# Weight rounding, decay shift and key factor of the input projection on ScalarE instead of GpSimd

## The chip, the cores and the metric

The kernel runs on one core of one Trainium2 chip. The core has a matrix engine (TensorE, PE in the profile, with its weight loads PEld in a row of their own), VectorE (DVE), ScalarE (ACT), GpSimd (POOL), and SyncE (SP), which here only issues DMAs. The metric is the device time of one execution in microseconds.

## The reference

One layer of a hybrid diffusion backbone on 128 context tokens and 1024 latent tokens, model width 1024. All of it is float32:

```python
h = rmsnorm(x, ln1_g) * (1 + sc1) + sh1
r, k, v, xw, xa, xg, xb, gb = split(h @ w_in)
decay = exp(-0.6065 * sigmoid(w0 + tanh(xw) @ w_up))   # for two directions
a     = sigmoid(a0 + xa @ a_up)                        # for two directions
kk    = unit_norm_per_head(k * k_k)
k_dir = k * (1 + (a - 1) * k_a)
ya = rwkv7_scan(r, decay, kk, kk * a, k_dir, v)        # 8 heads x 64, both directions
yb = rglru_scan(conv(xb)) * gelu(gb)                   # 8 blocks x 64, both directions
x  = x + g1 * (concat(ya, yb) @ w_out)
x  = x + g2 * ((gelu(ua) * ub) @ w_down)               # ua, ub = conv(rmsnorm(x) ... @ w_up)
```

## The kernel before

All 1152 tokens are handled as one sequence of columns. A float32 product is made of three matrix products (`mm3`): each operand is split into a part rounded to the matrix engine's narrower format (`hi`, made by `round_hi`) and the rest (`lo`, made by `rest_lo`), and hi·hi, hi·lo and lo·hi are added up.

**Input projection.** The columns of `w_in` are taken in 22 tiles of 128 columns, in the order of the list `ORDER`: 12 (xw and xa), then the tiles of k, r and v in turn, three tiles of the gate, and later those of the LRU. `win_load` fetches a tile as two pieces `win` of 128x512; `win_parts` (line 702) makes `winp`, hi and lo, from each piece, with one `round_hi` and one `rest_lo` of 128x512. `winp` has two buffers. `wtile` prepares tile i+1 when tile i begins, so its roundings wait until the last matrix product of tile i-1 has read its buffer. `proj` then runs 3 x 8 x 3 products per tile over three spans of 384 tokens, into two PSUM banks, which ScalarE empties.

**Beside it** run several generators, stepped by `beside` at set rates between pieces of 12 products. `stage_ab(f)`, for each of four head pairs f, works on six groups: two directions of a piece of 128 tokens and twice 512. A group goes through `rates` (two small products, two tanh on ScalarE into `b1` and `s`), `keys`, `powers` (two exponentials on ScalarE), `scaled_keys` (four products on VectorE), and `products` (the small matrix products `dg`, emptied by ScalarE). `keys`, the function that the diff touches, does in its order: shift of the decay `s` (0.5 s + 0.5), factor of the keys `kd` (b1 times a per-partition number plus another), `b1` on VectorE, `kd` times k on GpSimd, and the running sum of `s` on VectorE. `inverse` (lines 497 and 499) is a chain of some 60 short VectorE products for each f; `unit_keys` norms the keys.

The order of the instructions on each engine is fixed when the program is built: a planner goes through them by their place in the program and by its own estimates of when operands are ready. So the order on an engine can differ from the program's; on GpSimd the factor `kd` (line 596) mostly stands ahead of the shift of `s` (line 595). Each engine then works through its own list strictly in turn, and waits at an instruction whose operands or buffer aren't ready.

After the groups and inverses end, at about 460 us, a second stage runs the recurrence in two lanes beside the rest of the projection (`rest_of_projection`), then come the output projection and the feed-forward network.

Of the kernel before, what the change touches and what calls it, by code (L numbers as in the profile page):

```python
# [10 lines left out]
AF = mybir.ActivationFunctionType  # L11
OP = mybir.AluOpType
# [46 lines left out]
def tile_hybrid_step(  # L59
# [9 lines left out]
    V, A, G, PE = nc.vector, nc.scalar, nc.gpsimd, nc.tensor  # L69
# [33 lines left out]
    def round_hi(eng, hi, src):  # L103

        if eng is A:
            A.activation(hi, src, AF.Copy)  # L106
        else:
            eng.tensor_scalar(hi, src, 1.0, 0.0, op0=OP.mult, op1=OP.add)  # L108

    def rest_lo(eng, lo, src, hi):  # L110

        eng.tensor_tensor(lo, src, hi.bitcast(F32), op=OP.subtract)  # L112

    def vhalf(n, d):

        return n if d == 0 else 1 - n
# [4 lines left out]
    def const(name, *shape):  # L121
        return cp.tile(list(shape), F32, name=name)
# [60 lines left out]
    def ag(name):  # L183
        return abp.tile([128, 512], F32, name=name, tag="ag", bufs=NAG)
# [11 lines left out]
    def x8(name, dt=F32):  # L196
        return s1.tile([128, 2, D], dt, name=name, tag="x8", bufs=2)
# [50 lines left out]

    ln_half = const("ln_half", 128, 1)
    V.memset(ln_half, -0.6931471805599453)  # L250
    hsel = const("hsel", 128, 2)
    V.memset(hsel, 0.0)
    V.memset(hsel[0:64, 0:1], 1.0)
# [34 lines left out]
    def col(name, i, n=1):  # L288
        o = off[name] + i
        return colA[:, o:o + n]  # L290
# [5 lines left out]
    def scaled(name, src, n, mul, add=0.0):  # L296
        t = const(name, 128, n)
        V.tensor_scalar(t, src, mul, add, op0=OP.mult, op1=OP.add)
        return t

    nka = scaled("nka", col("rw_k_a", 0, 4), 4, -1.0)
    oka = scaled("oka", nka, 4, 1.0, 2.0)
# [102 lines left out]
    for b in range(4):  # L405
# [7 lines left out]
        for m in (2 * b, 2 * b + 1):  # L413
            ht = t4("ht")
            for q, (a, e) in enumerate(((0, 128), (128, T))):
                A.activation(ht[:, a:e], xT[b][:, m % 2, a:e], AF.Identity, scale=A1[:, m, q:q + 1],
                             bias=modc[:, m, q:q + 1])
# [138 lines left out]
    def stage_ab(f):  # L556
# [4 lines left out]
        class Group:  # L561
# [30 lines left out]
            def keys(self):  # L592
                W, b1, s = self.W, self.b1, self.s
                self.kd = ag("kd")[:, 0:W]
                G.tensor_scalar(s, s, 0.5, 0.5, op0=OP.mult, op1=OP.add)
                G.tensor_scalar(self.kd, b1, nka[:, f:f + 1], oka[:, f:f + 1], op0=OP.mult, op1=OP.add)
                V.scalar_tensor_tensor(b1, b1, -1.0, self.kk, op0=OP.add, op1=OP.mult)
                G.tensor_tensor(self.kd, self.kd, self.k, op=OP.mult)
                V.tensor_tensor_scan(s, keep[:, 0:W], s, 0.0, op0=OP.mult, op1=OP.add)
# [55 lines left out]
        for tg, (a, b) in enumerate(((0, 128), (128, 640), (640, T))):  # L655
            data = []
            for src in (r_d, k_d, kk_d):
                t = ag("rk")[:, 0:b - a]
# [43 lines left out]
    def win_parts(raw):  # L702
        w = x8("winp", F32R)
        hi, lo = w[:, 0], w[:, 1]
        for i, t in enumerate(raw):
            c = slice(512 * i, 512 * i + 512)
            round_hi(G, hi[:, c], t)
            rest_lo(V, lo[:, c], t, hi[:, c])
        return [a.rearrange("p (k c) -> p k c", k=8) for a in (hi, lo)]

    def wtile(m):
        i = ORDER.index(m)
        for a, q in enumerate(ORDER[i:i + 3]):
            if q not in win_raw:
                win_raw[q] = win_load(q)
            if a < 2 and q not in win_q:
                win_q[q] = win_parts(win_raw[q])
        return win_q[m]
# [294 lines left out]
    for h in range(2):  # L1013
        r = half(h)
        for d in range(2):
            for n in range(2):
                s = vhalf(n, d)
# [713 lines left out]
    if True:  # L1731
# [17 lines left out]
        f = zf.rearrange("p i k t -> p (i k t)")  # L1749
# [108 lines left out]
```

## Time and profile before

| | |
|---|---|
| median of 3 runs | 1878.95 us (1877.78 to 1882.11) |
| profiled execution, time | 1878.41 us |
| profiled execution, span | 1876.7 us |
| mean granted TensorE clock | 0.943 |
| PE busy | 1740.1 us (93%) |
| DVE busy | 1286.3 us (69%) |
| ACT busy | 814.9 us (43%) |
| POOL busy | 793.0 us (42%) |

Busy time is summed over the span. PE counts as busy while products overlap in its pipeline. [...]

### The profile page before, as it was taken

What the parts mean: (1) busy time and instruction counts of PE and PEld (TensorE: products, weight loads), DVE (VectorE), ACT (ScalarE), POOL (GpSimd) and SP (SyncE); (2) the same over time, 40 slices, a digit from 0 to 9 for tenths busy, and PEclk for the clock granted to TensorE, in tenths of its full rate; (3) what the DMA queues carried; (4) which work ended last, traced back from release to release, by engine and by line L of the source; (5) the groups of instructions that cost most, each with busy time, mean ns of one, the idle gap of its engine ahead of it and who ended that gap; (6) DMA issues with size and microseconds to landing.
All of it is one profiled execution on the core that took longest, in us unless ns stands there. A gap on an engine that the chain in (4) does not pass through costs nothing.

```text
span 1876.7 us, 35779 instructions
## 1 busy us (share of the span) xinstructions
PE 1740.1 (93%) x13341; PEld 1458.6 (78%) x13341; DVE 1286.3 (69%) x2632; ACT 814.9 (43%) x1695; POOL 793.0 (42%) x834
## 2 busy tenths in 40 slices
PE   5989998988899999789997889999999999999996
PEld 4766676778778778456675689999999999788885
DVE  6456977788466774357778966667776678566764
ACT  6344544441466567334334854444444443121211
POOL 2053636432253554131112076666666664334340
PEclk8897889888999999899998989999999999999998
DMA  9243535442434333676776312222222225648581
GB/s 295 62 155 124 159 124 175 132 150 81 144 101 143 112 104 97 218 234 216 248 236 222 130 53 84 76 71 77 71 71 78 76 71 165 188 150 271 167 256 59
DMA packets 268429, 264.93 MB, mean 141 GB/s; under 512 B 21173, under 2 KB 218448, under 8 KB 268256
## 3 DMA queue, kind: packets, MB, share of 16 engines
q1 hardware_dynamic: 252496, 245.97, 41.6%
q10 hardware_dynamic: 15472, 16.54, 2.6%
q8 instruction: 105, 1.72, 0.4%
q14 instruction: 68, 0.56, 0.1%
q0 software_dynamic: 288, 0.14, 0.0%
HBM read 188.00 MB, written 74.58 MB: 140 GB/s over the span
## 4 chain that ended last, share of the span: by engine, by line
PE 70%; DVE 12%; issue 6%; DMA 4%; ACT 4%; POOL 3%; SPq 0%; ACTq 0%; POOLq 0%; DVEq 0%
PE acc L92 13%; PE mm L92 10%; PE x L92 7%; PE y L92 7%; PE z L92 7%; PE v L92 3%; PE wo L92 3%; PE md L92 2%; PE lg L92 2%; PE ya L92 2%; DVE gt L497 2%; DVE X L499 2%; PE pa L92 2%; PE yb L92 1%; PE ca L92 1%
## 5 line engine op out<-in xcount | busy, mean ns | idle before, releaser
L92 PE MATMUL mm<-h_hi,winp 128*128 128x384 f32 x1056 | 315.0, 369 | 4.4 <-DVE vr L806 3.0
L92 PEld LDWEIGHTS mm<-h_hi,winp 128*128 128x128 f32 x1056 | 206.9, 204 | 26.3 <-issue 15.5
L92 PE MATMUL mm<-h_lo,winp 128*128 128x384 f32 x528 | 193.8, 367 | 2.9 <-DVE h_lo L112 2.9
L112 POOL TENSOR_TENSOR wl<-raw,wh 128x512 fp32r<-128x512 f32 x110 | 154.2, 1404 | 69.8 <-ACT wh L106 69.8
L106 ACT ACTIVATE wh<-raw 128x512 fp32r<-128x512 f32 x110 | 69.3, 632 | 146.7 <-PE z L92 80.4
L92 PEld LDWEIGHTS mm<-h_lo,winp 128*128 128x128 f32 x528 | 107.6, 204 | 10.9 <-issue 5.1
L92 PE MATMUL x<-f_hi,wh 128*128 128x256 f32 (+1 forms) x352 | 106.0, 301 | 8.7 <-ACT q L1650 5.0
L1088 POOL TENSOR_TENSOR BK<-BK,pc 128x256 f32<-128x256 f32 x72 | 47.4, 660 | 154.7 <-PE pa L92 56.7
L92 PE MATMUL x<-f_lo,wh 128*128 128x256 f32 (+1 forms) x352 | 105.7, 300 | 0.2 <-DVE f_lo L112 0.2
L92 PE MATMUL x<-f_hi,wl 128*128 128x256 f32 (+1 forms) x352 | 105.5, 300 | 0.0
L92 PE MATMUL y<-t_hi,wh 128*128 128x320 f32 (+1 forms) x352 | 105.0, 298 | 0.4 <-DVE q L1655 0.4
L92 PE MATMUL y<-t_lo,wh 128*128 128x320 f32 (+1 forms) x352 | 104.8, 298 | 0.0
L92 PE MATMUL y<-t_hi,wl 128*128 128x320 f32 (+1 forms) x352 | 104.7, 298 | 0.0
L112 POOL TENSOR_TENSOR wl<-S,wh 128x512 fp32r<-128x512 f32 x44 | 57.9, 1315 | 105.1 <-ACT wh L106 105.1
L108 POOL TENSOR_SCALAR winp<-win 128x512 fp32r<-128x512 f32 x44 | 31.9, 740 | 151.3 <-PE mm L92 104.6
L92 PE MATMUL acc<-f_hi 128*128 128x512 f32 x330 | 90.2, 395 | 2.5 <-ACT zf L1758 2.5
L108 POOL TENSOR_SCALAR t_hi<-raw 128x512 fp32r<-128x512 f32 x66 | 55.2, 839 | 78.5 <-PE acc L92 37.4
L1617 DVE SCALAR_TENSOR_TENSOR zf<-C,fcw,zf 128x567 f32<-128x567 f32 x66 | 63.7, 964 | 24.0 <-ACT zf L1615 24.0
L92 PEld LDWEIGHTS x<-f_hi,wh 128*128 128x128 f32 x352 | 68.1, 193 | 9.7 <-ACT q L1650 5.6
L92 PEld LDWEIGHTS acc<-f_hi 128*128 128x128 f32 x330 | 62.7, 191 | 16.0 <-ACT zf L1758 2.9
L112 DVE TENSOR_TENSOR t_hi<-raw,t_hi 128x512 fp32r<-128x512 f32 x66 | 48.3, 738 | 36.1 <-POOL t_hi L108 36.1
L1615 ACT ACTIVATE zf<-C,colB,fcw 128x576 f32<-128x576 f32 x66 | 57.2, 867 | 30.8 <-DVE C L1687 16.9
(514 smaller groups left out, 5248.5 us busy)
## 6 DMA issues: line engine op xcount, KB each, us to landing
raw<-in_w_down SPq DMA_DIRECT2D x132, 256.0 KB, 3.2
raw<-in_w_up SPq DMA_DIRECT2D x88, 256.0 KB, 3.0
wmod<-in_w_mod SPq DMA_DIRECT2D x68, 256.0 KB, 4.2
act_d<-zf SPq DMA_DIRECT2D x44, 288.0 KB, 2.3
src<-act_d SPq DMA_DIRECT2D x66, 192.0 KB, 3.6
win<-in_w_in SPq DMA_DIRECT2D x44, 256.0 KB, 3.5
KR<-kb_d SPq DMA_DIRECT2D x36, 256.0 KB, 3.3
VS<-v_d SPq DMA_DIRECT2D x36, 256.0 KB, 3.7
```

Of the source, the lines that this page charges most:

```text
L92: PE.matmul(out, lhsT, rhs, start=start, stop=stop, skip_group_check=True)
L106: A.activation(hi, src, AF.Copy)
L108: eng.tensor_scalar(hi, src, 1.0, 0.0, op0=OP.mult, op1=OP.add)
L112: eng.tensor_tensor(lo, src, hi.bitcast(F32), op=OP.subtract)
L497: V.tensor_tensor(tv, X[:, q + 1:32, q:q + 1].to_broadcast([128, m, q]), X[:, q:q + 1, 0:q].to_broadcast([128, m, q]), op=OP.mult)
L499: V.tensor_tensor(X[:, q + 1:32, 0:q], X[:, q + 1:32, 0:q], tv, op=OP.add)
L1088: G.tensor_tensor(bk, bk, pc_f[q.f][:, :, x:x + 1].to_broadcast([128, 2, 128]), op=OP.mult)
L1615: A.activation(u, src, AF.Identity, scale=fcw[:, 1, m:m + 1], bias=colb("ffn_conv_b", m))
L1617: V.scalar_tensor_tensor(dv[:, :, 1:64], sv[:, :, 0:63], fcw[:, 0, m:m + 1], dv[:, :, 1:64], op0=OP.mult, op1=OP.add)
```

## The change

A column of 0.5 (`p_half`) is written once by VectorE. In `keys` the shift of the decay and the factor of the keys become ScalarE activations (Identity with a scale and a bias); the factor's scale and bias are columns, one number for each partition, as before, the shift's bias is the new column. In `win_parts` the rounding of the weights becomes a ScalarE copy (`round_hi` has a branch for it). The rests `rest_lo` stay on VectorE, and the product of `kd` with k stays on GpSimd. All other uses of `round_hi` stay as they were.

```diff
+    p_half = const("p_half", 128, 1)
+    V.memset(p_half, 0.5)
...
             def keys(self):
                 W, b1, s = self.W, self.b1, self.s
                 self.kd = ag("kd")[:, 0:W]
-                G.tensor_scalar(s, s, 0.5, 0.5, op0=OP.mult, op1=OP.add)
-                G.tensor_scalar(self.kd, b1, nka[:, f:f + 1], oka[:, f:f + 1], op0=OP.mult, op1=OP.add)
+                A.activation(s, s, AF.Identity, scale=0.5, bias=p_half)
+                A.activation(self.kd, b1, AF.Identity, scale=nka[:, f:f + 1], bias=oka[:, f:f + 1])
                 V.scalar_tensor_tensor(b1, b1, -1.0, self.kk, op0=OP.add, op1=OP.mult)
                 G.tensor_tensor(self.kd, self.kd, self.k, op=OP.mult)
                 V.tensor_tensor_scan(s, keep[:, 0:W], s, 0.0, op0=OP.mult, op1=OP.add)
...
         for i, t in enumerate(raw):
             c = slice(512 * i, 512 * i + 512)
-            round_hi(G, hi[:, c], t)
+            round_hi(A, hi[:, c], t)
             rest_lo(V, lo[:, c], t, hi[:, c])
```

## Rows read from the trace of the kernel before

**Rows 1.** Windows: busy us (count) of PE, PEld, DVE, ACT, POOL; PEclk, DMA share, GB/s.

```profile
120.00:140.00 20.00, 14.77 (x181) 9.54 (x180) 14.98 (x16) 8.38 (x19) 18.06 (x17) 0.98 0.60 187
...
280.00:300.00 20.00, 18.39 (x261) 13.56 (x260) 16.16 (x18) 11.58 (x28) 16.49 (x18) 0.94 0.65 211
...
60.00:460.00 400.00, 362.20 (x3498) 284.56 (x3497) 294.52 (x578) 170.04 (x401) 162.09 (x214) 0.87 0.42 132
```

**Rows 2.** Waits of all engines, 60 to 460 us: total us, times, longest.

```profile
POOL winp L108 <- PE mm L92: 104.4, 11, 19.4
...
ACT P L605 <- DVE s L599: 39.4, 19, 6.0
...
PE dg L92 <- DVE bk L620: 13.0, 8, 3.1
...
DVE b L597 <- POOL kd L596: 8.3, 5, 4.4
...
DVE s L599 <- POOL s L595: 7.5, 5, 3.8
```

**Rows 3.** Groups of instructions of POOL, whole span: count, busy us, mean ns.

```profile
L108 POOL TENSOR_SCALAR winp<-win 128x512 fp32r<-128x512 f32 x44 | 31.9, 740 | 151.3 <-PE mm L92 104.6 <-DMA win<-in_w_in 32.3 <-issue 14.3
...
L596 POOL TENSOR_SCALAR kd<-b,nka,oka 128x512 f32<-128x512 f32 (+1 forms) x24 | 24.2, 1007 | 43.8 <-ACT b L587 42.1 <-PE ab L92 1.6
...
L595 POOL TENSOR_SCALAR s<-s 128x512 f32<-128x512 f32 (+1 forms) x24 | 15.4, 641 | 1.2 <-ACT s L590 1.2
```

**Rows 4.** Groups of instructions of ACT, whole span, same columns.

```profile
L106 ACT ACTIVATE wh<-raw 128x512 fp32r<-128x512 f32 x110 | 69.3, 632 | 146.7 <-PE z L92 80.4 <-PE y L92 58.2 <-DMA raw<-in_w_up 6.4
...
L606 ACT ACTIVATE s<-s,ln_half 128x512 f32<-128x512 f32 (+1 forms) x24 | 14.6, 609 | 0.3
...
L416 ACT ACTIVATE ht<-xT,modc,A 128x128 f32<-128x128 f32 (+1 forms) x16 | 12.9, 858 | 3.6 <-DVE h_lo L112 3.6
```

**Rows 5.** Windows, POOL busy (count) of lines 595, 596 and 108, in this order.

```profile
280.00:300.00 20.00, 1.68 (x2) 0.94 0.65 211
...
280.00:300.00 20.00, 3.56 (x2) 0.94 0.65 211
...
280.00:300.00 20.00, 0.00 (x0) 2.10 (x2) 0.94 0.65 211
```

**Rows 6.** Timeline of 302 to 314 us: start, duration, instruction, idle before it.

```profile
302.96 1.15 POOL L596 TENSOR_SCALAR kd<-b,nka,oka 128x512 f32<-128x512 f32 x1
303.37 0.68 ACT L590 ACTIVATE s<-ab,w0h 128x512 f32<-128x512 f32 x1
...
304.20 1.59 POOL L598 TENSOR_TENSOR kd<-kd,rk 128x512 f32<-128x512 f32 x1
304.57 1.76 DVE L620 TENSOR_TENSOR bk<-b,s 128x512 f32<-128x512 f32 x1
...
305.75 1.06 POOL L595 TENSOR_SCALAR s<-s 128x512 f32<-128x512 f32 x1
...
307.27 2.30 DVE L599 TENSOR_TENSOR_SCAN s<-keep,s 128x512 f32<-128x512 f32 x1
...
309.61 0.63 ACT L605 ACTIVATE P<-s 128x512 f32<-128x512 f32 x1 [4.29 <-DVE s L599]
...
313.79 0.51 PE L92 MATMUL dg<-kr,bk 64*32 64x64 f32 x13 [2.97 <-DVE bk L620]
```

**Rows 7.** Timeline of 388 to 393 us: one running sum.

```profile
390.82 1.21 DVE L599 TENSOR_TENSOR_SCAN s<-keep,s 128x512 f32<-128x512 f32 x1
```

**Rows 8.** Groups of instructions of DVE by shape, 60 to 460 us.

```profile
L599 DVE TENSOR_TENSOR_SCAN s<-keep,s 128x512 f32<-128x512 f32 x16 | 26.6, 1663 | 7.3 <-POOL s L595 7.3
```

**Rows 9.** Timeline of 37 to 73 us, ACT and POOL.

```profile
44.34 0.88 POOL L108 TENSOR_SCALAR winp<-win 128x512 fp32r<-128x512 f32 x1
44.84 3.31 ACT L416 ACTIVATE ht<-xT,modc,A 128x128 f32<-128x128 f32 x4 [0.79 <-DVE h_lo L112]
...
72.52 0.48 ACT L736 ACTIVATE xwt<-mm 64x384 f32<-64x384 f32 x1 [3.51 <-PE mm L92]
72.57 0.62 POOL L108 TENSOR_SCALAR winp<-win 128x512 fp32r<-128x512 f32 x1 [19.42 <-PE mm L92]
```

## Prediction

> **What bounds the kernel now.** I first read the busy times in windows, to find the stage the change lives in, then the waits of all engines there, then the groups of the instructions that move, and last the timeline around two stalls.
>
> The moved work lies between 37 and about 700 us, most of it between 60 and 460. In those 400 us PE is busy 362.2 us, so it stands still for 37.8; DVE is busy 294.5, ACT 170.0 and POOL 162.1 [rows 1]. The averages hide bursts. When a group goes through `keys` and `powers`, POOL is the fullest engine: 18.06 of 20 us from 120 to 140, and 16.49 of 20 from 280 to 300, while ACT has 8.38 and 11.58 [rows 1]. The reader is to see that the bursts, not the average of 40%, are where POOL could hold others up.
>
> The waits say how far it does. DVE waits for the key factor 8.3 us in 5 cases and for the shifted decay 7.5 us in 5 [rows 2]. These two are direct. The end of the same chain is where PE stalls: the small products `dg` wait 13.0 us in 8 cases for the last of the scaled keys [rows 2]. PE stalled is time lost, because PE has nearly no slack in this stage: what is lost there is mostly lost at the end. ACT for its part sits idle 39.4 us, in 19 cases, until the running sum ends [rows 2]; this is room for new work, if it comes at the right time.
>
> **What moves, and its cost.** From POOL go 44 roundings (31.9 us), 24 factors (24.2) and 24 shifts (15.4), together 71.5 us [rows 3].
>
> ACT gets them. A rounding of 128x512 on ACT has rows of its own kind: 632 ns [rows 4], so 44 cost 27.8 us. A shift is like the second exponential, which has the same 24 pieces and one column operand: 14.6 us for all [rows 4]. The factor has two column operands, and no row has just that shape. Below it lies the same 14.6 us; above it 24 times the 858 ns of line 416, which has two column operands and 576 columns on average against 384 here [rows 4], 20.6 us. I take 17, between the two. ACT thus gets some 59 us, and a group gets (14.6 + 17) / 24 = 1.3 us on average. One column of 0.5 is written by DVE once, ahead of the projection; I put it at nothing, and a tenth of a microsecond would be its size.
>
> In the window from 280 to 300 the three lines hold POOL for 1.68 + 3.56 + 2.10 = 7.34 us [rows 5]. POOL falls there from 16.49 to about 9.2. ACT rises from 11.58 by two shifts, two factors and two roundings: about 2 x 1.5 + 1.3 = 4.3 at the length of the large pieces, to about 15.9 of 20. So the burst is not emptied, its load changes engine. What is gained is order: on POOL the shift of one group stood behind its factor and its key product.
>
> **A stall worked through.** At 302 us the second of two groups is in `keys`. POOL does the factor from 302.96 on, the key product from 304.20, and the shift only at 305.75, to 306.81; the tanh that the shift needs had ended on ACT at 304.05 [rows 6]. The running sum goes from 307.27 to 309.57, the exponential starts at 309.61, and PE waits 2.97 us before the `dg` at 313.79 [rows 6]. With the change ACT, idle there for 4.29 us [rows 6], does the shift from 304.05 and the factor behind it, so both are done by about 305.6. `b` on DVE can't start before line 620 ends at 306.33 [rows 6], or, if DVE is less disturbed, some 0.7 us sooner, and the running sum follows by 0.7 us. It would then start at 306.3 to 307.0 instead of 307.27. What it lasts is the other half: 2.30 us here, beside POOL's work, and 1.21 us alone [rows 6, 7]. The key product, now a microsecond later on POOL, can still fall beside it. The exponential thus starts 0.3 to 2.1 us sooner, and of the stall of 2.97 us a tenth to seven tenths go. I take half, a little above the middle, because in the burst from 280 to 300 two roundings stand in POOL's list as well [rows 5]: over the 13.0 us of such stalls [rows 2], **-6.5 us**. Bounds: none of it (0) and all of it (-13.0).
>
> **DVE beside POOL.** The 16 running sums of 512 columns take 1663 ns on average [rows 8] against 1.21 us for one alone [rows 7], 7.2 us over all. The moved pieces are 71.5 us, some 63 of them in the window from 60 to 460, of POOL's 162.1 there [rows 1, 3], four tenths; four tenths of 7.2 is 2.9 us. Where DVE has been the last to end (the inverses, towards 460 us) such time comes back, where PE is, it does not; I take half, **-1.4 us**, bounds 0 and -2.9.
> [...]
>
> **The roundings in ACT's list.** A rounding waits until PE has read the buffer two tiles back; on POOL these waits were 104.4 us in 11 cases [rows 2] and hurt nobody. On ACT they could hold up what stands behind them: the emptying of PSUM (lines 780, 792, 805) and the DMAs of k, r and v that ACT's queue issues. But the wait is the same that ACT keeps anyway: at 72.52 ACT starts the last emptying of a tile, released by PE's product, and at 72.57 POOL starts its rounding, released by the same [rows 9]. A pair costs 1.26 us; its rest on VectorE and PE need it only a tile later. I put the roundings at nothing, covered by that tile; without the cover, each pair would cost 1.26 us, for the 16 pairs from 60 to 460 us 20 us. At the very start the first tiles are prepared while ACT makes the normed input `ht`: at 44.34 POOL rounds, at 44.84 ACT goes on after 0.79 us of idle time [rows 9]. One rounding of 0.63 us nearly fits, another may stand ahead of `ht`: **+0.6 us**, bounds 0 and +2.5 (four roundings).
>
> **What else waits on ACT.** ACT's other work in a burst (tanh of the next group, emptying of `dg` and of PSUM) comes behind 1.3 us more for each group. I take **+1 us** for it, bounds 0 and the third rival.
>
> Sum: -6.5 - 1.4 + 0.6 + 1 = -6.3 us against the profiled execution's 1878.41 us: **1872 us**. That execution is 0.5 us under the median of the runs, which moves nothing here. I take no term for TensorE's clock. [...]
>
> **Rivals.**
>
> *Nothing to see.* The stalls of PE stay because DVE, with 294.5 us of work and in bursts full, would have ended as late anyway; ACT at 15.9 of 20 us is as full as POOL was at 16.5. The half that I took then is nothing: 1878 us. For it speaks that DVE's idle time put down to POOL is only 15.8 us of 400 [rows 2]; against it that PE's waits end at this chain. [...]
>
> *DVE is let go.* If the chain over DVE is what ends last throughout, all its waits for POOL go (8.3 + 7.5 = 15.8 us [rows 2]) and the running sums get 2.9 us back: -18.7, **1860 us**. Against it: some of these waits lie where PE was not waiting.
>
> *ACT becomes the chain.* Slower. Now the exponential `P` starts as soon as the running sum ends: ACT is idle before it in 19 cases [rows 2]. If the planner puts the next group's shift and factor, or a pair of roundings, ahead of it in ACT's list, `P` starts up to 1.3 us later, or 2.6 with roundings, and with it all the scaled keys, `dg` and the inverse. At the 8 stalls of PE that is 8 x 1.3 = 10.4 us: **1889 us**. It decides from the point where `P` starts on average over half a group's share, 0.65 us, after the sum. For it speaks that ACT's list is in strict turn and the planner doesn't know the chip's true times; against it that shift and factor are ready before the sum ends.
>
> **How the numbers follow.** A change under 0.2% (3.8 us) is about what runs of this kernel can't tell from none. Chances: forecast 0.38, nothing to see 0.21, DVE let go 0.13, ACT as the chain 0.28. Faster is 0.38 + 0.13, less a little of the forecast that ends near the bound: 0.50; same 0.22; slower 0.28. The forecast's own range goes from all of its gains without its costs (-15.9) to a quarter of the stalls with them (-3.25 + 1.6): 1862 to 1877. The range reaches to both far rivals, 1858 to 1889, and leaves out a fifth: of each of them the outer part.
>
> **What would show it.** Right: POOL busy between 60 and 460 near 100 us, ACT near 222; DVE's waits for `kd` and `s` under 5 us together; `dg` waiting on line 620 for 6 to 7 us; the second stage begins some 6 us sooner. The forecast is wrong if ACT's idle time before `P` is replaced by DVE waiting for `P`, if PE waits for ACT's emptying, or if the planner's new order opens other stalls of PE of the same size elsewhere.

## The result, and the profile after

The changed kernel takes 1851.88 us (median of 4 runs, 1849.17 to 1858.53), the kernel before on the same chip 1878.37 us. The ratio is 0.9865, with a 95% interval of 0.9827 to 0.9902: 26.5 us faster by the medians. The forecast was 1872 us, with a range from 1858 to 1889. The direction is right; the gain is four times the forecast, and the time lies outside the range.

The profiled execution took 1849.17 us, its span is 1847.5 us, its mean granted clock, as a share of full speed, 0.954 (before 0.943). PE is busy 1716.4 us, DVE 1272.2, ACT 865.5, POOL 721.8. All lines from `keys` on stand two lower in the file: the shift is L597, the factor L598, `b` L599, the key product L600, the running sum L601, the exponential `P` L607, the last scaled keys L622.

The windows that answer to [rows 1], same columns:

```profile
120.00:140.00 20.00, 19.36 (x205) 13.01 (x204) 17.33 (x23) 15.27 (x34) 8.14 (x11) 1.00 0.68 217
60.00:460.00 400.00, 364.81 (x3826) 292.51 (x3827) 292.81 (x612) 222.08 (x495) 107.94 (x147) 0.91 0.44 140
```

In the burst from 120 to 140 us PE goes from 14.77 to 19.36 busy us, POOL from 18.06 to 8.14, ACT from 8.38 to 15.27. Over the 400 us ACT is at the 222 us that the prediction named and POOL at 107.9 (named: 100). PE's idle time there is 35.2 us against 37.8, 2.6 us less; but the granted clock, the third number from the end, is 0.91 against 0.87. That is the first sign of where the gain lies.

The moved instructions on ACT (groups, whole span, columns as in [rows 4]):

```profile
L106 ACT ACTIVATE winp<-win 128x512 fp32r<-128x512 f32 x44 | 26.6, 624 | 0.2
...
L598 ACT ACTIVATE kd<-b,oka,nka 128x512 f32<-128x512 f32 (+1 forms) x24 | 16.8, 700 | 0.0
L597 ACT ACTIVATE s<-s,p_half 128x512 f32<-128x512 f32 (+1 forms) x24 | 14.7, 611 | 0.1
```

26.6, 16.8 and 14.7 us; the prediction took 27.8, 17 and 14.6. These prices hold.

The waits that answer to [rows 2], 60 to 460 us:

```profile
POOL kd L600 <- ACT kd L598: 96.8, 20, 16.5
...
DVE s L601 <- ACT s L597: 26.3, 7, 10.0
...
DVE b L599 <- ACT kd L598: 11.0, 4, 4.8
...
PE ab L92 <- POOL kd L652: 9.0, 5, 3.1
...
PE iv L92 <- DVE T L506: 5.9, 4, 2.6
...
ACT P L607 <- DVE s L601: 3.9, 5, 1.3
...
PE dg L92 <- DVE bk L622: 1.9, 5, 0.6
```

and two lines of before that [rows 2] do not show:

```profile
PE iv L92 <- DVE T L504: 3.1, 2, 2.7
...
PE ab L92 <- POOL kd L650: 2.0, 1, 2.0
```

The stalls of PE before `dg` are down from 13.0 to 1.9 us. ACT hardly idles before `P` any more (39.4 to 3.9 us); it is busy 222.1 us in this stretch instead of 170.0. DVE now waits more for `s` and `kd` than before (37.3 against 15.8 us), and PE's stalls ahead of `dg` are down all the same. Stalls that the prediction had not counted have grown: the bonus products `ab` wait 9.0 us for GpSimd, against 2.0 us in the trace of before, and the products `iv` of the inverse 5.9 us against 3.1.

**Where the time went.** The last product with the input weights ends at 752.9 us before and at 724.0 us after, 28.9 us sooner, and the difference at the end of the span is 29.2: behind that point nothing is gained or lost. The windows from 37 us to that point, before and then after:

```profile
37.00:752.90 715.90, 659.87 (x6225) 522.88 (x6226) 491.03 (x980) 358.76 (x776) 300.06 (x366) 0.90 0.40 125
```

```profile
37.00:724.00 687.00, 637.62 (x6226) 508.76 (x6226) 475.55 (x979) 408.08 (x868) 230.29 (x274) 0.93 0.42 130
```

PE is idle 715.9 - 659.9 = 56.0 us before and 687.0 - 637.6 = 49.4 after, 6.6 us less. What the lower clock level took is the window times (1 - granted clock): 71.6 us before, 48.1 after, 23.5 us less (each within 3.6, as the clock is printed to two places). Together 30.1, against 28.9 measured. In this pair of executions, then, some 23 us are time that the lower clock no longer takes, and 7 us are stalls.

Single executions vary in this. For all runs the span and the mean granted clock are known, so each span splits into span x (1 - clock), the *clock part*, and the rest. Over 101 runs of the kernel before the clock part is 100.5 us and the rest 1775.9; over the 4 runs of the changed kernel 87.9 and 1763.2. By the runs, the clock part gives **12.6 us** and the rest **12.7 us**. The clock parts of the four runs lie between 83.2 and 98.4 us, so the 12.6 carry a standard error of some 3.6 us.

**One place, read closely.** Most of the lead is made in the first burst: the sixth weight tile's first product starts at 166.5 us before and at 149.0 after. By the windows from 37 us to there (PE busy 116.30 and 105.00 us, granted clock 0.86 and 0.92) some 6 of these 17.5 us are idle time and some 9 the lower clock; the rest, some 2 us, goes with work put off, as the changed kernel has done 746 products by then and the kernel before 815. Windows of before, then of after:

```profile
120.00:130.00 10.00, 7.83 (x42) 5.23 (x47) 7.24 (x9) 4.00 (x8) 9.50 (x9) 1.00 0.45 145
130.00:140.00 10.00, 6.94 (x150) 4.32 (x149) 7.74 (x8) 4.37 (x11) 8.56 (x9) 0.95 0.74 229
140.00:150.00 10.00, 8.59 (x55) 4.77 (x54) 4.73 (x8) 5.79 (x14) 3.20 (x5) 0.67 0.53 168
150.00:160.00 10.00, 10.00 (x68) 7.02 (x61) 5.51 (x8) 4.43 (x13) 4.82 (x6) 0.52 0.22 75
```

```profile
120.00:130.00 10.00, 10.00 (x103) 6.97 (x103) 8.29 (x10) 6.32 (x15) 5.42 (x7) 1.00 0.53 163
130.00:140.00 10.00, 9.36 (x104) 6.04 (x102) 9.04 (x14) 8.95 (x20) 2.72 (x5) 1.00 0.83 271
140.00:150.00 10.00, 9.32 (x104) 6.20 (x103) 6.88 (x11) 8.61 (x18) 5.14 (x5) 1.00 0.40 129
150.00:160.00 10.00, 9.48 (x118) 8.72 (x118) 7.49 (x12) 5.75 (x13) 1.88 (x2) 1.00 0.57 179
```

Two timelines of these places, before and after:

```profile
129.92 0.81 PE L92 MATMUL dg<-kr,bk 64*32 64x64 f32 x64 [2.17 <-DVE bk L620]
...
131.25 3.39 DVE L112 TENSOR_TENSOR winp<-win,winp 128x512 fp32r<-128x512 f32 x2
131.42 0.63 ACT L605 ACTIVATE P<-s 128x512 f32<-128x512 f32 x1 [5.98 <-DVE s L599]
...
134.56 0.68 DVE L616 TENSOR_TENSOR kr<-rk,P 128x512 f32<-128x512 f32 x1
...
137.19 0.94 PE L92 MATMUL dg<-kr,bk 64*32 64x64 f32 x64 [3.06 <-DVE bk L620]
```

```profile
131.70 0.68 DVE L622 TENSOR_TENSOR bk<-b,s 128x512 f32<-128x512 f32 x1
132.30 1.28 DVE L112 TENSOR_TENSOR winp<-win,winp 128x512 fp32r<-128x512 f32 x2
```

Before, PE stands still for 2.17 us ahead of the `dg` at 129.92 and 3.06 us ahead of the one at 137.19, and then the granted clock falls to 0.67 and 0.52. In windows of 1 us the clock of before reads 1.00 up to 139 us, 0.50 from 140 to 142 and from 146 to 159, and 1.00 again from 160. These two levels are the only ones in the traces of before and after, so the time at half clock is twice the clock part. The second slice lies nearly all at half clock: PE reads "10.00 busy" from 150 to 160, but with 68 products, where the other kernel does 118 (not all of one size). The two stalls themselves are 5.2 us; the low clock behind them costs up to 10 x (0.33 + 0.48) = 8.1 us more, an estimate that takes PE to have work all the time. After, PE has no idle time over 0.4 us between 124 and 146 us, and the clock stays at 1.00.

The timelines also show how a rounding can reach PE. In the second stall DVE does the two rests of a weight tile, 3.39 us long, from 131.25 on; `P` has ended at 132.05, but the scaled keys `kr` start only at 134.56. In the changed kernel the two rests take 1.28 us and stand behind the last scaled keys `bk`.

In this burst the clock of before falls after stalls of 2.17 and 3.06 us. The experiments below show that it can't be read off the sum of the stalls: rounds_wait has stalls of 1.01 and 2.32 us ahead of `dg` in this burst, and its clock stays at 1.00. Two of its windows:

```profile
130.00:140.00 10.00, 6.75 (x95) 4.93 (x94) 8.56 (x13) 7.88 (x21) 5.08 (x8) 1.00 0.76 252
140.00:150.00 10.00, 10.00 (x107) 6.92 (x107) 7.36 (x11) 5.45 (x11) 6.71 (x8) 1.00 0.38 120
```

### The profile page after: what moved, and what is told of

It reads as the page before. It is cut to its first block, busy times and chain, and to the rows that moved or that the text cites. A ratio compares the mean times of both kernels' runs of the same rounds, so it can differ in the third digit from the quotient of the medians.

```text
span 1847.5 us, 35759 instructions
## 1 busy us (share of the span) xinstructions
PE 1716.4 (93%) x13341; PEld 1442.9 (78%) x13341; DVE 1272.2 (69%) x2633; ACT 865.5 (47%) x1787; POOL 721.8 (39%) x742
## 4 chain that ended last, share of the span: by engine, by line
PE 66%; DVE 9%; ACT 3%; DMA 3%; issue 3%; POOL 3%; SPq 0%; ACTq 0%; POOLq 0%; DVEq 0%
PE acc L92 14%; PE x L92 7%; PE y L92 7%; PE z L92 7%; PE mm L92 7%; PE v L92 3%; PE wo L92 3%; PE ya L92 2%; PE lg L92 2%; PE md L92 2%; PE pa L92 2%; PE ca L92 1%; DVE X L501 1%; PE yb L92 1%; DVE gt L499 1%
## 5 line engine op out<-in xcount | busy, mean ns | idle before, releaser
L92 PE MATMUL mm<-h_hi,winp 128*128 128x384 f32 x1056 | 304.4, 358 | 4.9 <-DVE vr L808 3.2
L92 PEld LDWEIGHTS mm<-h_hi,winp 128*128 128x128 f32 x1056 | 198.7, 196 | 26.4 <-issue 14.9
L92 PE MATMUL mm<-h_lo,winp 128*128 128x384 f32 x528 | 187.7, 356 | 3.0 <-DVE h_lo L112 3.0
L92 PEld LDWEIGHTS mm<-h_lo,winp 128*128 128x128 f32 x528 | 103.7, 197 | 9.6 <-DVE h_lo L112 4.5
L112 DVE TENSOR_TENSOR t_hi<-raw,t_hi 128x512 fp32r<-128x512 f32 x66 | 48.1, 735 | 37.0 <-POOL t_hi L108 37.0
L600 POOL TENSOR_TENSOR kd<-kd,rk 128x512 f32<-128x512 f32 (+1 forms) x24 | 32.2, 1342 | 97.0 <-ACT kd L598 96.8
```

The source lines that it names most:

```text
L92: PE.matmul(out, lhsT, rhs, start=start, stop=stop, skip_group_check=True)
```

## The experiments

All have 5 rounds beside the kernel before (its medians in the five sets of runs: 1876.01, 1879.17, 1878.05, 1878.00 and 1878.26). "Clock part" and "rest" are the differences from the 101 runs of before, worked out as above, in us; their standard errors are 1.4 to 3.6 us for the clock part and 0.8 to 1.9 for the rest.

| kernel | median us (runs) | ratio [95%] | clock part | rest |
|---|---|---|---|---|
| the whole change | 1851.88 (4) | 0.9865 [0.9827, 0.9902] | -12.6 | -12.7 |
| keys_only | 1880.56 (12) | 1.0029 [1.0004, 1.0055] | +7.2 | -2.8 |
| rounds_only | 1861.03 (6) | 0.9902 [0.9870, 0.9935] | -12.5 | -4.6 |
| shift_only | 1864.21 (6) | 0.9916 [0.9884, 0.9948] | -9.3 | -5.2 |
| factor_only | 1876.60 (12) | 0.9991 [0.9967, 1.0015] | -1.1 | -0.1 |
| shift_rounds | 1851.97 (6) | 0.9860 [0.9824, 0.9896] | -15.0 | -10.3 |
| after_pool | 1862.44 (6) | 0.9904 [0.9876, 0.9931] | -8.7 | -7.9 |
| rounds_pool | 1869.59 (12) | 0.9951 [0.9926, 0.9976] | -5.4 | -4.0 |
| rounds_wait | 1863.18 (6) | 0.9923 [0.9896, 0.9950] | -11.2 | -4.5 |
| before_late | 1868.38 (10) | 0.9942 [0.9916, 0.9967] | -5.0 | -5.7 |
| keys_late | 1876.67 (12) | 0.9980 [0.9957, 1.0003] | -1.8 | 0.0 |
| rounds_late | 1865.45 (9) | 0.9941 [0.9916, 0.9967] | -1.7 | -9.9 |
| after_late | 1862.46 (6) | 0.9912 [0.9886, 0.9938] | -9.6 | -5.7 |
| after_swap | 1853.74 (6) | 0.9870 [0.9839, 0.9901] | -10.9 | -12.5 |
| after_first | 1869.64 (9) | 0.9944 [0.9919, 0.9970] | -1.9 | -6.0 |
| after_rest | 1874.23 (12) | 0.9984 [0.9964, 1.0005] | +4.1 | -7.2 |
| before_fill | 1888.01 (12) | 1.0054 [1.0023, 1.0085] | -6.0 | +16.2 |

### The parts by themselves

Shift and factor on ScalarE, the roundings left on GpSimd:

```diff
-G.tensor_scalar(s, s, 0.5, 0.5, op0=OP.mult, op1=OP.add)
-G.tensor_scalar(self.kd, b1, nka[:, f:f + 1], oka[:, f:f + 1], op0=OP.mult, op1=OP.add)
+A.activation(s, s, AF.Identity, scale=0.5, bias=p_half)
+A.activation(self.kd, b1, AF.Identity, scale=nka[:, f:f + 1], bias=oka[:, f:f + 1])
```

> Only the shift of the decay and the factor of the keys are on ScalarE; the roundings of the projection's weights stay on GpSimd. Theory chain (the way from the tanh to the running sum got shorter): at least three quarters of the gain of 25 us, 1853 to 1860 us. [...]

The roundings alone:

```diff
-            round_hi(G, hi[:, c], t)
+            round_hi(A, hi[:, c], t)
```

> Only the roundings of the projection's weights are on ScalarE; shift and factor stay on GpSimd. Theory chain: a gain of no more than 5 us, 1873 to 1879 us, since no rounding lies between tanh and running sum. Theory GpSimd time: 31.9 of 71.5 us are taken off, 45% of the gain, about 1867 us. [...]

The shift alone (the first pair of lines of keys_only), and the factor alone (the second pair):

> Only the shift of the decay is on ScalarE. It comes last in GpSimd's list and the running sum needs it at once. Theory chain: more than half of what shift and factor give together, 1862 to 1870 us. Theory GpSimd time: 15.4 of 71.5 us, a fifth of the gain, about 1873 us.

> Only the factor of the keys is on ScalarE. It stands ahead of the shift in GpSimd's list, so the shift comes sooner too. Theory chain: as much as the shift alone or more, 1860 to 1870 us. Theory GpSimd time: 24.2 of 71.5 us, a third of the gain, about 1870 us.

Shift and roundings, the factor left on GpSimd:

> Rounding and shift on ScalarE, the factor of the keys left on GpSimd. If the parts add up, the gains of the two alone (17 and 15 us) come together, 32 us, some 6 us more than the whole change. If each only takes away the same time at the low clock and the same waits, it gains no more than the whole change: 17 to 26 us.

The two edits of the chain of the keys together gain nothing, though they take away just the stalls that the prediction lived on. PE's waits in keys_only, 60 to 460 us:

```profile
PE ab L92 <- POOL kd L652: 12.4, 5, 3.3
PE ab L92 <- DVE bon L485: 8.7, 4, 3.7
PE ab L92 <- POOL P L606: 4.7, 2, 2.6
...
PE dg L92 <- DVE bk L622: 2.3, 3, 1.2
```

`dg` is at 2.3 us instead of 13.0, and three waits of the bonus products, 25.8 us together, have come up in its place. The roundings alone gain 17 us and leave the `dg` stalls as they were (12.8 us in 8 cases):

```profile
PE dg L92 <- DVE bk L620: 12.8, 8, 3.4
```

Shift and roundings without the factor are as fast as the whole change. The parts do not add up: 17 and 15 us alone, 26 together. Of the theories, the chain (the shorter way from the tanh to the running sum) fits shift_only alone, and GpSimd's time (each microsecond taken off GpSimd counts alike, which gives about 1865 us for keys_only) fits none of the four. The theory of the clock, that the time falls by half of what the time at half clock before 480 us falls by (126 us before, 89 in the changed kernel), comes near for rounds_only: the granted clock up to 480 us is 0.90 against 0.87, which is about 29 us less at half clock, so 14 us, and 17 were measured. For keys_only (0.88) it gives 5 us, and there is no gain.

### GpSimd kept full

The changed kernel, with GpSimd given one-input instructions into an unused tile for the work that it lost. The written order of the other engines' instructions stays nearly that of the changed kernel: laid side by side, the traces' lists of PE's 13341 instructions differ in 41 lines, against 623 between before and after.

```diff
+    dum = constp("dum", 128, 256)
...
                 A.activation(s, s, AF.Identity, scale=0.5, bias=p_half)
+                n = min(W, 256)
+                for _ in range(3 if W == 512 else 2):
+                    G.tensor_scalar(dum[:, 0:n], self.r[:, 0:n], 0.5, 0.5, op0=OP.mult, op1=OP.add)
...
             round_hi(A, hi[:, c], t)
+            if m < 13 or m in (18, 19, 20):
+                for n in (256, 128):
+                    G.tensor_scalar(dum[:, 0:n], t[:, 0:n], 0.5, 0.5, op0=OP.mult, op1=OP.add)
```

> The changed kernel, with GpSimd given as much work again as was taken from it: for each group in keys three passes over 256 columns (two over 128 for the small groups) and for each weight piece up to tile 20 one over 256 and one over 128, all from data of the same moment into a scratch tile that nothing reads. The lists of PE, VectorE and ScalarE stay nearly the same as in the changed kernel. [...] Theory clock and order (what counts is that PE is not held up, and with it the clock): 1852 to 1860 us, with time at half clock before the end of the projection near 99 us.

POOL is busy 161.46 us from 60 to 460 us, as before the change (162.09). Its gain is 0.96% where that of the changed kernel is 1.35%: three tenths go, 7 us, and 17 to 18 us stay. Its 1862.44 us lie between the 1852 to 1860 us of the theory of clock and order and the 1870 us or more that it would take if the fuller GpSimd cost the time. The same for the roundings alone:

```diff
             round_hi(A, hi[:, c], t)
+            if m < 13 or m in (18, 19, 20):
+                for n in (256, 128):
+                    G.tensor_scalar(dum[:, 0:n], t[:, 0:n], 0.5, 0.5, op0=OP.mult, op1=OP.add)
```

> The rounding alone on ScalarE, and GpSimd given back as much time as that takes from it, in instructions that write an unused tile; the order on the other engines is practically that of the kernel with the rounding alone, which gained 17 us. If the emptier GpSimd is what the rounding gains by, the gain goes back to 0 to 5 us. If the order and the place of the rounding are, it stays at 13 to 17 us; by the share of the rounding in what the full GpSimd took from the whole change (8.5 us by 32 of 71 us of instructions) it is 13 us.

Half of the gain goes, 0.49 of 0.98%, which lies between the two expectations. In both pairs a fuller GpSimd costs 7 to 9 us in nearly the same written order, each known only to some 8 us either way, as the intervals of a pair overlap. By these sizes the rest of the gain is not a matter of how full GpSimd is.

GpSimd's list given back the wait for the weight buffer, with next to no work:

```diff
+            if i == 0:
+                G.tensor_scalar(hi[:, 0:8], t[:, 0:8], 1.0, 0.0, op0=OP.mult, op1=OP.add)
             round_hi(A, hi[:, c], t)
```

> The rounding alone on ScalarE, but GpSimd writes the first 8 columns of each weight tile's rounded half ahead of it, so that GpSimd's list waits for the buffer as before, with next to no work. If that wait in GpSimd's list is what the rounding's move takes away, the gain of 17 us goes: 1873 to 1880 us. If it hurt nobody, as the prediction says, the time stays that of the rounding alone, 1861 us, within the 4 to 10 us that a new order is worth.

The first of GpSimd's waits in this kernel, 60 to 460 us:

```profile
POOL winp L708 <- PE mm L92: 104.2, 11, 20.1
```

The wait is back (104.4 us in [rows 2]), and the gain stays, 15 of 17 us. So the gain of rounds_only does not come from this wait's going. A harm of a few us is not ruled out: the written order is another as well (225 lines of PE's list in the trace differ from rounds_only).

### The same work in another written order

The planner writes one order for all engines, and any edit changes it everywhere. To see what order alone is worth, the bonus sums are drained one step later, with no work added, removed or moved:

```diff
                 g.keys()
                 yield
-                for _ in late:
-                    yield
...
                 g.scaled_keys()
                 yield
+                if d == 1:
+                    for _ in late:
+                        yield
```

On the kernel before, on keys_only, on rounds_only and on the changed kernel:

> The kernel before with its bonus sums drained one step later (after the scaled keys of the next piece's second group instead of its keys); no instruction is added, removed or put on another engine, but the planner writes another order for all engines. If the time follows what each engine has to do, it stays within 3 us of the kernel before. If the written order alone is worth as much as the edits tried so far, it differs from the kernel before by more than 4 us, to either side, as the same move cost the changed kernel about 10 us and gained the kernel with both keys on ScalarE about 6 us.

> Shift and factor on ScalarE, roundings on GpSimd, and the bonus drained later, as in the run before. With shift and factor alone PE no longer stalls for the scaled keys (2.3 us instead of 13.0) but for the bonus (12.4 and 8.7 us), and no time is gained. Theory order (the bonus moved ahead in PE's list took back what the shorter chain gave): 1855 to 1866 us. Rival (the roundings on GpSimd hold the chain up whatever stands in PE's list): 1872 to 1882 us.

> The rounding alone on ScalarE, with the bonus sums drained one step later; to be set against the kernel before with that same move (1868 us). In the four pairs so far that differ in the rounding alone, its move gained 0.56 to 1.64%. If it gains in any order, this run gives 1838 to 1859 us. If those gains were a matter of the order that came with it, it can lie on either side of 1868 us.

> The changed kernel, but the bonus of a piece (two products on GpSimd, then small products on PE) is drained after the scaled keys of the next piece's second group, not before the exponentials of its first. In the changed kernel PE stalls 9.0 us in 5 cases for the second of these products. Theory clock: without these stalls PE is denser, time at half clock falls below 99 us, and the time to 1840 to 1848 us. Rival: the stalls only move to other small products, 1850 to 1856 us.

And the changed kernel with factor and shift exchanged:

```diff
-A.activation(s, s, AF.Identity, scale=0.5, bias=p_half)
 A.activation(self.kd, b1, AF.Identity, scale=nka[:, f:f + 1], bias=oka[:, f:f + 1])
+A.activation(s, s, AF.Identity, scale=0.5, bias=p_half)
```

> The changed kernel with ScalarE doing the factor of the keys ahead of the shift of the decay. If the chain from the decay to the powers sets the time, the scan starts later by one factor (0.82 us) in the 16 large groups, which costs 0 to 13 us. If the order that the planner writes is what moves the time, it can come out on either side of the changed kernel, by up to 10 us.

The same move gains 0.58% on the kernel before and 0.49% on keys_only, costs 0.39% on rounds_only and 0.48% on the changed kernel. The exchange of factor and shift costs 0.05%, no difference that can be measured. Of the four, the gains on the kernel before and on keys_only are clear of noise, the cost on the changed kernel just so, that on rounds_only not quite. Order alone is thus worth up to 11 us, nearly twice the gain that was forecast.

Two of these runs were aimed at the bonus products, and neither gave the time that their theory had. In after_late their wait for GpSimd is down from 9.0 to 2.8 us, but 1862.46 us is slower than even the rival had it, and `dg` waits 10.5 us. In keys_late it is down from 12.4 to 2.8 us, that for `bon` from 8.7 to 1.4; the time is still that of the kernel before (ratio 0.9980), as the rival had it, and the stalls ahead of `dg` are back:

```profile
PE dg L92 <- DVE bk L622: 15.4, 10, 3.8
...
PE ab L92 <- POOL kd L652: 2.8, 1, 2.8
```

It also gives pairs of kernels in which one thing differs. The roundings' move, by the quotients of the ratios: -0.98% (on before), -0.56% (on shift_only), -1.64% (on keys_only), -0.68% (on keys_late), and -0.01% on before_late, where 1838 to 1859 us had been expected and 1865 came. Each is known to 0.3 to 0.5%. Mean of the five -0.77%, some 14 us with a standard error of 5, but in one order nothing. The move of shift and factor: +0.29, -0.37, +0.38 and -0.29%, mean 0.0.

### By place

The change made up to the first burst alone, and from there on alone:

```diff
-                G.tensor_scalar(s, s, 0.5, 0.5, op0=OP.mult, op1=OP.add)
-                G.tensor_scalar(self.kd, b1, nka[:, f:f + 1], oka[:, f:f + 1], op0=OP.mult, op1=OP.add)
+                if f == 0:
+                    A.activation(s, s, AF.Identity, scale=0.5, bias=p_half)
+                    A.activation(self.kd, b1, AF.Identity, scale=nka[:, f:f + 1], bias=oka[:, f:f + 1])
+                else:
+                    G.tensor_scalar(s, s, 0.5, 0.5, op0=OP.mult, op1=OP.add)
+                    G.tensor_scalar(self.kd, b1, nka[:, f:f + 1], oka[:, f:f + 1], op0=OP.mult, op1=OP.add)
...
-            round_hi(G, hi[:, c], t)
+            round_hi(A if ORDER.index(m) < 6 else G, hi[:, c], t)
```

(after_rest has `f > 0` and `>= 6`.)

> The change made only up to the first of the four bursts of key work (shift and factor of that burst, roundings of the first six weight tiles); from there on GpSimd does them as before. [...]

> The complement: the first burst as in the kernel before, the change made from the second burst on. If the gain is made where the trace of the changed kernel shows it, this kernel has no lead at the start of the sixth tile, shows the stalls and the low clock of the first burst, and gains the other 8 to 12 us: 1866 to 1870 us, so that the two runs add up to the whole change. If the written order is what matters, they need not add up: from 1851 to 1881 us.

The first burst of after_first is like that of the changed kernel, and that of after_rest is as expected. after_first starts its sixth tile at 148.7 us, 17.8 us ahead of before; a lead that lasted would have given 1859 to 1863 us. after_rest starts it at 162.5 us, with the old stalls (1.99 and 3.07 us ahead of `dg`) and the low clock behind them:

```profile
120.00:130.00 10.00, 8.01 (x94) 5.50 (x94) 9.48 (x9) 3.77 (x7) 9.51 (x9) 1.00 0.59 193
130.00:140.00 10.00, 5.66 (x88) 3.86 (x86) 7.01 (x10) 4.46 (x14) 6.66 (x7) 1.00 0.60 184
140.00:150.00 10.00, 8.24 (x69) 3.57 (x69) 5.07 (x8) 5.19 (x12) 5.39 (x7) 0.69 0.43 140
150.00:160.00 10.00, 10.00 (x116) 8.24 (x116) 4.59 (x12) 6.47 (x17) 2.04 (x3) 0.80 0.40 131
```

But the lead is not kept. after_first has 9.0 us of it left at the end of the input weights (743.9 against 752.9 us): two tiles that before passes in 56 us (230.6 to 286.5) take it 66.5 us (211.6 to 278.1). Part of that is work put off until then, 811 products in this stretch against 566. But the changed kernel has 812 there and needs 59.0 us (209.0 to 268.0): its clock is 0.88 against 0.83, and PE stands still for 1.7 us against 7.7, with a wait of 3.6 us for `bon` among them. And after_rest gains 4 us by its median where 8 to 12 were expected. Together 12 us, not 26. The expectation that the lead of one place can be added up is refuted.

### Products to fill PE's stalls

The kernel before with four unused products of 128x512 ahead of the `dg` of each large group, 64 in all:

```diff
                 dgb = [bank("dg"), bank("dg")]
+                for _ in range(4 if nx == 8 else 0):
+                    mm(dgb[0][:, 0:512], h_hi[0][:, 0, 0:128], h_hi[0][:, 0, 0:512])
```

> [...] Theory clock (PE's thin stretches bring the clock down and that is the greater part of the loss): time at half clock falls from 147 us by 30 or more, and the time does not rise, 1862 to 1876 us. Rival (the stalls cost only themselves, the clock falls for other reasons): time at half clock stays within 15 us of 147, and the time rises to 1878 to 1890 us.

The clock part falls by 6.0 us (standard error 3), that is, 12 us less at half clock, and the rest rises by 16.2, of which 14.5 us would be the 64 products themselves: an estimate from the 227 ns by which products of 128x512 follow each other at full clock in the trace of before (18 of them in 4.24 us from 1608.96 us on). So the rival's forecast came true, and the theory's fall of 30 us or more did not. PE isn't less idle either: it is busy 357.12 us from 60 to 460 us in this trace, against 362.20. Whether fuller stalls give clock back is not shown by this run.

## Why the prediction was wrong

**The prices held, and the stalls ahead of `dg` went.** 58.1 us arrived on ACT (named: 59). `dg` gave back 11.1 of its 13.0 us where half was taken, -6.5. But DVE's waits for `kd` and `s`, which were to fall under 5 us, rose to 37.3, and a sign of being wrong came about, other stalls of PE from the new order: PE's idle time from 60 to 460 us fell by 2.6 us in all. That the direction came out right is luck: shift and factor, on which the forecast rests, gain nothing by themselves (keys_only), and the move that it put at nothing gains most.

**The step that failed is what those stalls were worth, and it failed three times over.**

*The clock.* "I take no term for TensorE's clock." This term is about half of the gain, 12.6 of 25.3 us over the runs. [Rows 1] had the PEclk of 0.87 for the stage, and the windows of 10 us above show a way from POOL to it: POOL at 9.50 and 8.56 of 10 us, DVE's scaled keys late, PE stalled behind them, the clock down behind the stalls. The prediction looked at the burst and at the average of the clock, and not at the 20 us after the burst. But stalls and clock are not proportional. The windows of rounds_only:

```profile
60.00:460.00 400.00, 362.18 (x3815) 292.97 (x3816) 294.81 (x592) 191.89 (x442) 144.19 (x189) 0.91 0.43 137
```

PE is busy 362.18 us, the same as before the change (362.20), with the same stalls at `dg`; yet the clock is 0.91 instead of 0.87, and 12.5 of its 17 us are clock. rounds_late is the reverse: 9.9 us from the rest and 1.7 from the clock. What decides where the clock falls, beyond that in the first burst of before it falls after two stalls of PE, is not settled here.

*The chain.* The gain was laid to shift and factor. By themselves they give nothing. In keys_only PE runs into other waits, the bonus products behind GpSimd's `kd` and `P` and behind `bon` (25.8 us); the whole change has 9.0 us of the first of them left. That these waits are the cause is not shown: with them nearly gone in keys_late, the `dg` stalls are back and the time is still that of the kernel before. Taking one stall away opened another, and why shift alone gains 15 us and shift with factor nothing stays open.

*The roundings.* "I put the roundings at nothing." As a cost on ACT that is right, and with their wait back in GpSimd's list 15 of the 17 us stay. But their leaving is the part that gains most: 17 us alone, 14 in the mean over five orders. When GpSimd is kept full, half of it goes back (rounds_pool). The prediction took the rest of a rounding on VectorE to be covered by a tile; in the first burst of before two rests stand ahead of the scaled keys in a stall of 3.06 us. That is not the whole of it, as rounds_only has a stall of 3.38 us in the same burst with one rest of 0.66 us ahead of them. Which of GpSimd's instructions come late for whom was not settled: in after_pool PE's wait for GpSimd's `kd` is 12.5 us instead of 9.0 and that of the inverse `iv` for DVE 8.2 instead of 5.9, from 60 to 460 us; with a clock part 3.9 us higher that is about the size, but no run takes these waits apart.

**DVE beside POOL: right in kind, too small.** It was put at 2.9 us for the running sums, of which half was taken. Groups of DVE from 60 to 460 us, after:

```profile
L601 DVE TENSOR_TENSOR_SCAN s<-keep,s 128x512 f32<-128x512 f32 x16 | 23.4, 1460 | 26.3 <-ACT s L597 26.3
L112 DVE TENSOR_TENSOR winp<-win,winp 128x512 fp32r<-128x512 f32 x33 | 23.1, 714 | 11.8 <-ACT winp L106 11.7
L599 DVE SCALAR_TENSOR_TENSOR b<-b,rk 128x512 f32<-128x512 f32 x16 | 21.0, 1314 | 6.6 <-ACT kd L598 6.3 <-DMA rk<-kk_d 0.3
L618 DVE TENSOR_TENSOR kr<-rk,P 128x512 f32<-128x512 f32 x16 | 12.5, 783 | 3.1 <-issue 1.7 <-ACT P L607 1.3
...
L622 DVE TENSOR_TENSOR bk<-b,s 128x512 f32<-128x512 f32 x16 | 10.9, 681 | 0.0
```

and before, beside [rows 8]:

```profile
L112 DVE TENSOR_TENSOR winp<-win,winp 128x512 fp32r<-128x512 f32 x30 | 26.3, 893 | 9.8 <-POOL winp L108 9.8
L620 DVE TENSOR_TENSOR bk<-b,s 128x512 f32<-128x512 f32 x16 | 16.6, 1040 | 0.0
...
L616 DVE TENSOR_TENSOR kr<-rk,P 128x512 f32<-128x512 f32 x16 | 14.7, 917 | 4.5 <-ACT P L605 4.5
L597 DVE SCALAR_TENSOR_TENSOR b<-b,rk 128x512 f32<-128x512 f32 x16 | 14.4, 897 | 8.3 <-POOL kd L596 8.3
```

The running sums fall by 3.2 us, as the bound had it. The rests of the weights (893 to 714 ns, 5.4 us for 30), `bk` (5.7) and `kr` (2.2) fall too, and `b` rises by 6.6: GpSimd's key product now starts up to 0.51 us ahead of it in 7 of 16 cases, and these take 1.52 to 1.77 us; before, in 2 of 16, with 1.76 and 1.80 us. The sum of these five groups is -9.9 us of DVE time, three times the bound. In the trace of before, a running sum of this shape takes 1.21 to 1.23 us where POOL is idle beside it (6 of 16) and 1.19 to 2.32 us where it is busy; `bk` takes 0.68 us with POOL idle (4 of 16) and 0.68 to 1.77 us beside it. But after_pool has the groups of the scan, the rests, `b`, `kr` and `bk` at 1513, 726, 1222, 826 and 723 ns with POOL as busy as before: these times do not follow from how busy POOL is over the stretch.

**The rivals.** *Nothing to see* is refuted: the roundings cost 740 ns on GpSimd and 624 on ACT, and their move still gained the most; the price of the instruction says little about the price of its place. *ACT becomes the chain* did not come about: ACT's idle time ahead of `P` fell, and DVE's wait for `P` is 2.3 us. In keys_only other stalls of PE came up, as in that rival, but behind GpSimd's bonus and not behind ACT. *DVE is let go* was nearest in size (1860 us), but not by its mechanism: DVE waits longer for `s` and `kd` than before.

**What of the 26 us belongs to the moved work?** Three kernels with the work of the changed one, or with it but the factor, in other orders take 1862.46, 1853.74 and 1851.97 us. The sum of the mean gains over the orders tried is 0.77% + 0.0%, 14 us with a standard error of 5 or more; by this estimate the rest, some 11 us, came with the order that the planner happened to write. No version tried is faster than the changed kernel by more than the intervals allow; shift_rounds (1851.97) is its equal with one instruction less moved.

## What to carry to other kernels

Where PE has hardly any slack, follow each stall into the 20 us behind it: the granted clock there can cost more than the stall (up to 8.1 us behind 5.2 us here), and a total of stalls can stay while the clock changes. Before a gain of half a per cent is put down to an edit of a kernel whose order a planner writes, time the same work in another order: here that alone moved 7 to 11 us in four of five cases, and the edits' gains did not add up. When one wait is taken away, look for the stall that comes up in its place: here the bonus products stalled once the scaled keys did not, the scaled keys again once the bonus was moved, and neither was faster than the kernel before by more than the noise.

## What the hardware showed beyond that

The 101 runs of the kernel before, one and the same program in five sets on four chips, have a mean granted clock from 0.937 to 0.954 and take 1865.68 to 1892.35 us; the two go together (correlation -0.90, within each set -0.89 to -0.95; 1.28 us for each 0.001 of the clock). A span of 1876 us times 0.001 is 1.88 us, so some two thirds of the lost clock reaches the end. The clock thus differs between runs of the same instruction lists, and a single profile shows one draw of it: the profiled execution of before (0.943) lies below the mean of 0.9465, that of after (0.954) above its own 0.9525.

An activation of 128x512 from SBUF to SBUF has a price by its operands in this trace: 0.62 us for a copy, 0.72 with one column, 0.82 with two (means of the groups of this shape 624, 721 and 807 ns). Timeline of ACT after, start and duration:

```profile
123.84 0.82 ACT L598 ACTIVATE kd<-b,oka,nka 128x512 f32<-128x512 f32 x1
...
124.54 0.72 ACT L597 ACTIVATE s<-s,p_half 128x512 f32<-128x512 f32 x1
...
129.70 0.62 ACT L106 ACTIVATE winp<-win 128x512 fp32r<-128x512 f32 x1
```
